# A two-layer encoder trunk on one core, its instruction order planned on another timing simulator

## Chip, cores and metric

The kernel runs on one core of a Trainium2 chip. The metric is the device time of one execution in microseconds (us); the figures below are medians of several runs, and one profiled execution gives the trace. Five engines take instructions, each from a queue of its own and each in the order of that queue: TensorE (PE in the rows; PEld is its weight load), VectorE (DVE), ScalarE (ACT), GpSimd (POOL), and SyncE (SP), which here only issues DMAs. SPq, DVEq and so on in a row are the engine's own instruction queue.

## What is computed

The trunk has two layers over 512 frames of width 1024, in float32. Cut to what matters, for x of shape (512, 1024):

```
for i in (0, 1):
    h = even_mixer(x) if i == 0 else odd_mixer(x, positions)
    x = layer_norm(sqrt(2) * x + h)
    gu = x @ w_gate_up[i];  gate, up = gu[:, :2816], gu[:, 2816:]
    x = layer_norm(sqrt(2) * x + (silu(gate) * up) @ w_down[i])

even_mixer(x):
    p = x @ w_in                             # one projection for both head groups
    a = gated linear attention, 4 heads, chunks of 64 frames, gated state
    b = RWKV-7, 8 heads of 64: S_t = S_{t-1} diag(w_t) + (S_{t-1} a_t) b_t^T + v_t k_t^T, y_t = S_t r_t,
        group norm, bonus term, low-rank output gate
    return concat(a, b) @ w_out

odd_mixer(x, positions):
    q, kv = low-rank projections with rms_norm, rotary key shared by 16 heads
    s = (q k^T) * scale, masked by chunks of 64;  return (softmax(s) v) @ w_out
```

## The kernel before

The program is traced once, in straight line, with no loop on the chip: 21743 instructions in the trace. The tracing library sees tiles (`pool.tile`), works out every semaphore, and at the end orders the instructions itself. Its scheduler walks through a simulated execution: whenever an engine is free there, the engine takes, of the instructions whose inputs and buffers are ready in the simulation, the one that was traced first. So the code's order is a priority, and the simulator's clock decides when a later instruction may pass an earlier one. What comes out is one fixed list for each engine; on the chip nothing passes anything any more within a list. By the library's own description it has two such simulators. The default one leaves out the fixed cost of GpSimd's elementwise instructions; the other, a timeline simulator, is more detailed, and of the activation tables it sees no loads.

All large products are three matmuls each (`gemm3`, lines 185, 186 and 187): each float32 operand is split into a rounded high part (a copy on ScalarE, line 191 or 216) and the rest (VectorE, line 192, or GpSimd), or the rest is built by an accumulating DMA that GpSimd issues (lines 215, 1263 and 1506).

**The first stage** (`even_mixer`) is a set of generators that `weave` interleaves by hand-set costs: the input projections (`gemms`, `proj`: 25 blocks of 128 columns, 24 matmuls each, the matmuls `ps_g<-xh,wh`, `ps_g<-xl,wh`, `ps_g<-xh,wl` of lines 185 to 187), four RWKV streams of two heads each (`rwkv_prep`, `rwkv_chunks`, `rwkv_out`: many 64x64 matmuls, lines 520 to 780), the gated linear attention (`gla_scores` with line 870, `gla_states`, `gla_out`), and the output projection (`w_out`). In `rwkv_prep`, GpSimd multiplies and copies a tile (`e.R`, line 532, and `AR`, line 533). The ScalarE functions of this stage are pinned to table loads by explicit order edges (`behind`).

**The feed-forward stages** (`ffn`, line 1236) multiply by a Strassen-like scheme: for each of six column groups, products P1 to P7, each two token halves wide, whose results VectorE combines (line 1270); `turn` transposes the combined halves (line 1314) before the down projection (`down_ln`, lines 185 to 187 again). **The attention stage** (`mla`) computes scores (line 1617), transposes (line 1633) and value products (line 1646) two units behind one another, with the key and query projections as a background stream. Layer norms end each half layer (`Norm`, lines 1027 to 1036), and the last one writes the output (line 1038).

All pools are opened inside one `ExitStack` in `body`. `body` is called with the tile context open and nothing else is traced in it.

Of the kernel before, what the change touches and what calls it, by code (L numbers as in the profile page):

```python
# [1688 lines left out]
def body(tc, I, O, coff, voff, dbg=False):  # L1689
# [2 lines left out]
    g.table = None  # L1692
    g.nc, g.tc, g.I, g.O, g.dbg = nc, tc, I, O, dbg
    from contextlib import ExitStack
    with ExitStack() as es:
        cp = g.cp = es.enter_context(tc.tile_pool(name="cp", reuse_waits="tile", bufs=1))
        g.dp = es.enter_context(tc.tile_pool(name="dp", bufs=1, space=bass.MemoryType.DRAM))
        cst = cp.tile([P, I["cst"].shape[1]], F32, name="cst")
# [116 lines left out]
```

## Time and profile before

| | |
|---|---|
| median of 3 runs | 1392.69 us (1392.04 to 1393.3) |
| the profiled execution's own time | 1392.04 us |
| its span, first to last instruction | 1390.0 us |
| TensorE busy | 1339.4 us (96%) |
| VectorE busy | 920.7 us (66%) |
| ScalarE busy | 686.5 us (49%) |
| GpSimd busy | 233.4 us (17%) |
| granted TensorE clock, mean | 0.99 |

A matmul's record overlaps the next one's, so that TensorE's busy time says where it waited (busy is missing), and not how fast it ran. Times within the profile count from the first instruction of the span.

### The profile page before, as it was taken

What the parts mean: (1) busy time and instruction counts of PE and PEld (TensorE: products, weight loads), DVE (VectorE), ACT (ScalarE), POOL (GpSimd) and SP (SyncE); (2) the same over time, 40 slices, a digit from 0 to 9 for tenths busy, and PEclk for the clock granted to TensorE, in tenths of its full rate; (3) what the DMA queues carried; (4) which work ended last, traced back from release to release, by engine and by line L of the source; (5) the groups of instructions that cost most, each with busy time, mean ns of one, the idle gap of its engine ahead of it and who ended that gap; (6) DMA issues with size and microseconds to landing.
All of it is one profiled execution on the core that took longest, in us unless ns stands there. A gap on an engine that the chain in (4) does not pass through costs nothing.

```text
span 1390.0 us, 21743 instructions
## 1 busy us (share of the span) xinstructions
PE 1339.4 (96%) x8382; PEld 1060.7 (76%) x8382; DVE 920.7 (66%) x1704; ACT 686.5 (49%) x1212; POOL 233.4 (17%) x278
## 2 busy tenths in 40 slices
PE   8899999999999999999999999999999899999997
PEld 6577777766677788997888877666677788997886
DVE  3687677644496766667556367988785766667456
ACT  6653344455536455555344346555445455555341
POOL 2230021132311111127301220000001111120000
PEclk9999999989999999999999999999999999999999
DMA  7563343531478787763225321111367787773232
GB/s 243 114 125 60 74 100 72 105 65 46 145 221 198 157 189 166 151 125 97 91 93 157 109 94 47 53 55 46 117 163 190 155 193 167 145 127 93 91 107 90
DMA packets 74328, 168.15 MB, mean 121 GB/s; under 512 B 21232, under 2 KB 22384, under 8 KB 74096
## 3 DMA queue, kind: packets, MB, share of 16 engines
q0 software_dynamic: 21888, 60.83, 26.2%
q1 hardware_dynamic: 51808, 103.83, 22.6%
q10 hardware_dynamic: 528, 2.10, 0.4%
q8 instruction: 66, 1.08, 0.3%
q14 instruction: 38, 0.31, 0.1%
HBM read 163.77 MB, written 2.95 MB: 120 GB/s over the span
## 4 chain that ended last, share of the span: by engine, by line
PE 55%; DVE 4%; DMA 4%; issue 4%; ACT 2%; POOL 1%; SPq 0%; DVEq 0%; ACTq 0%; POOLq 0%
PE ps_g L1236 23%; PE ps_g L186 8%; PE ps_g L185 8%; PE ps_g L187 8%; PE ps_s L1617 3%; DMA raw<-in_w_gu 2%; PE ps_o L1646 2%; PE ps_t L1633 1%; PE ps_s L1314 1%; DMA wl<-in_w_mi 1%; DVE wl L192 1%; ACT wh L191 1%; DVE w L1270 0%; DMA w<-in_w_mo 0%; DVE x L1008 0%
## 5 line engine op out<-in xcount | busy, mean ns | idle before, releaser
L192 DVE TENSOR_TENSOR wl<-raw,wh 128x1024 fp32r<-128x1024 f32 (+1 forms) x116 | 127.6, 1111 | 87.7 <-ACT wh L191 87.7
L191 ACT CAST wh<-raw 128x1024 fp32r<-128x1024 f32 (+1 forms) x116 | 111.6, 967 | 140.7 <-PE ps_g L1236 94.9
L1263 POOL DMA_DIRECT2D raw<-in_w_gu x96 | 83.3, 869 | 496.9 <-DVE wl L192 274.0
L1236 PE MATMUL ps_g<-wh,xh 128*128 128x512 f32 (+1 forms) x312 | 115.9, 372 | 2.1 <-ACT wh L191 2.1
L187 PE MATMUL ps_g<-xh,wl 128*128 128x512 f32 (+2 forms) x296 | 113.2, 382 | 3.3 <-DMA wl<-in_w_even 2.2
L1236 PE MATMUL ps_g<-wh,xl 128*128 128x512 f32 (+1 forms) x312 | 114.8, 368 | 0.0
L185 PE MATMUL ps_g<-xh,wh 128*128 128x512 f32 (+2 forms) x296 | 114.6, 387 | 0.0
L186 PE MATMUL ps_g<-xl,wh 128*128 128x512 f32 (+2 forms) x296 | 113.3, 383 | 0.0
L186 PE MATMUL ps_g<-wl,ah 128*128 128x512 f32 x288 | 112.0, 390 | 0.6 <-DVE wl L192 0.6
L185 PE MATMUL ps_g<-wh,ah 128*128 128x512 f32 x288 | 111.7, 392 | 0.5 <-ACT ah L191 0.4
L187 PE MATMUL ps_g<-wh,al 128*128 128x512 f32 x288 | 110.8, 389 | 0.0
L192 DVE TENSOR_TENSOR wl<-w,wh 128x1024 fp32r<-128x1024 f32 (+2 forms) x79 | 89.4, 1132 | 31.9 <-ACT wh L191 31.4
L191 ACT CAST wh<-w 128x1024 fp32r<-128x1024 f32 (+2 forms) x79 | 76.3, 966 | 61.4 <-PE ps_g L186 36.5
L191 ACT CAST ah<-hid 128x512 fp32r<-128x512 f32 x72 | 43.7, 621 | 98.8 <-PE ps_g L186 98.8
L192 DVE TENSOR_TENSOR al<-hid,ah 128x512 fp32r<-128x512 f32 x72 | 49.4, 697 | 60.7 <-ACT ah L191 60.7
L1236 PE MATMUL ps_g<-wh,Sh 128*128 128x512 f32 (+1 forms) x232 | 87.1, 376 | 0.0
L1236 PE MATMUL ps_g<-wh,Sl 128*128 128x512 f32 (+1 forms) x232 | 86.7, 374 | 0.0
L1236 PE MATMUL ps_g<-wl,xh 128*128 128x512 f32 (+1 forms) x312 | 78.2, 372 | 4.1 <-DVE wl L192 4.1
L215 POOL DMA_DIRECT2D wl<-in_w_even x48 | 41.6, 867 | 227.0 <-ACT wl L214 191.9
L216 ACT CAST wh<-w 128x512 fp32r<-128x512 f32 x64 | 39.4, 618 | 81.2 <-PE ps_g L186 49.4
L187 PEld LDWEIGHTS ps_g<-xh,wl 128*128 128x128 f32 (+1 forms) x296 | 55.8, 189 | 14.9 <-DMA wl<-in_w_even 3.4
L1236 PEld LDWEIGHTS ps_g<-wh,xh 128*128 128x128 f32 x312 | 58.6, 188 | 10.6 <-ACT wh L191 3.2
(462 smaller groups left out, 3293.2 us busy)
## 6 DMA issues: line engine op xcount, KB each, us to landing
raw<-in_w_gu POOLq DMA_DIRECT2D x64, 512.0 KB, 5.6
w<-in_w_dn SPq DMA_DIRECT2D x44, 512.0 KB
raw<-in_w_gu SPq DMA_DIRECT2D x32, 512.0 KB
w<-in_w_even SPq DMA_DIRECT2D x48, 256.0 KB
wl<-in_w_even POOLq DMA_DIRECT2D x48, 256.0 KB, 4.7
raw<-in_w_gu POOLq DMA_DIRECT2D x32, 384.0 KB, 4.8
w<-in_w_gu SPq DMA_DIRECT2D x12, 512.0 KB
raw<-in_w_gu SPq DMA_DIRECT2D x16, 384.0 KB
```

Source lines behind the costliest of these rows:

```text
L185: nc.tensor.matmul(out, lhsT=wh, rhs=xh, start=first, stop=False)
L186: nc.tensor.matmul(out, lhsT=wh, rhs=xl, start=False, stop=False)
L187: nc.tensor.matmul(out, lhsT=wl, rhs=xh, start=False, stop=last)
L191: c = nc.scalar.copy(h, src)
L192: (eng or nc.vector).tensor_tensor(l, in0=src, in1=h, op=ALU.subtract)
L215: nc.gpsimd.dma_start(l, src, accum_op=ALU.add)
L216: nc.scalar.copy(h, w)
L1236: nc.tensor.matmul(acc[u][:, :n], lhsT=A_[a][:, k, P * u:P * u + P], rhs=w[:, q], start=first and k + a + b == 0, stop=k + b == 4, skip_gr ...
L1263: nc.gpsimd.dma_start(T[k][k2], w[r, q, k2], accum_op=ALU.add)
L1314: nc.tensor.transpose(out=p[:, m * P:(m + 1) * P], in_=y[:, m * P:(m + 1) * P], identity=g.C("ident"))
L1617: nc.tensor.matmul(p[:, :nk], lhsT=Q[:, h % 4, qb * P:(qb + 1) * P], rhs=K[:, h % 4, :nk], start=True, stop=True)
L1646: nc.tensor.matmul(o[64 * e:64 * e + 64, kb * P:], lhsT=Vv[:, kb, (h - 1 + e) * 64:(h + e) * 64], rhs=t[e][kb][:, kb * P:], start=kb == 0, ...
```

## The change

The whole body of the kernel is traced inside one block, and that block is scheduled on the timeline simulator in place of the default one. By the library's description a block is a basic block of its own, entered unconditionally and scheduled as a unit: nothing traced outside is scheduled in among its instructions. No operation, tile, buffer count or traced order is changed.

```diff
@@ -1692,7 +1692,7 @@
     g.table = None
     g.nc, g.tc, g.I, g.O, g.dbg = nc, tc, I, O, dbg
     from contextlib import ExitStack
-    with ExitStack() as es:
+    with tc.block(schedule_with_timeline_sim=True), ExitStack() as es:
         cp = g.cp = es.enter_context(tc.tile_pool(name="cp", reuse_waits="tile", bufs=1))
         g.dp = es.enter_context(tc.tile_pool(name="dp", bufs=1, space=bass.MemoryType.DRAM))
         cst = cp.tile([P, I["cst"].shape[1]], F32, name="cst")
```

## Rows read from the trace of the kernel before

**Rows 1.** The page's head: span, then busy us, share, instructions of each engine

```profile
span 1390.0 us, 21743 instructions
PE 1339.4 (96%) x8382; PEld 1060.7 (76%) x8382; DVE 920.7 (66%) x1704; ACT 686.5 (49%) x1212; POOL 233.4 (17%) x278
```

**Rows 2.** Busy time by stretches: us, each engine (instructions), TensorE clock, DMA share, GB/s

```profile
34.75:104.25 69.50, 62.11 (x379) 43.95 (x379) 49.32 (x98) 44.02 (x79) 20.36 (x26) 0.98 0.59 120
104.25:278.00 173.75, 168.96 (x2314) 128.61 (x2313) 120.59 (x297) 71.50 (x130) 25.91 (x33) 1.00 0.40 82
278.00:382.25 104.25, 102.49 (x903) 70.01 (x901) 47.76 (x99) 55.33 (x125) 32.09 (x31) 0.94 0.31 86
...
486.50:625.50 139.00, 139.00 (x714) 124.36 (x713) 92.04 (x116) 75.74 (x109) 25.47 (x30) 1.00 0.77 158
...
1112.00:1251.00 139.00, 139.00 (x716) 124.54 (x715) 91.79 (x115) 75.74 (x109) 25.13 (x29) 1.00 0.78 158
```

**Rows 3.** TensorE's waits, 0 to 420 us: who for whom, total us, times, longest

```profile
PE ps_c L520 <- ACT sq L518: 2.7, 1, 2.7
PE ps_l L870 <- DVE lvd L864: 2.2, 4, 1.4
...
PE ps_c L562 <- DVE sq L530: 2.1, 2, 1.8
PE ps_c L562 <- DVE Mrb L554: 1.5, 2, 1.1
PE ps_l L870 <- DVE big L873: 1.0, 1, 1.0
```

**Rows 4.** TensorE's waits, 420 to 1390 us

```profile
PE ps_s L1314 <- DVE w L1270: 7.1, 6, 1.3
```

**Rows 5.** TensorE in order of time, 208.8 to 213 us: start, us, what

```profile
209.35 0.39 PE L185 MATMUL ps_g<-xh,wh 128*128 128x512 f32 x1
211.12 1.15 PE L870 MATMUL ps_l<-lvd 64*64 64x64 f32 x32 [1.39 <-DVE lvd L864]
212.20 0.49 PE L186 MATMUL ps_g<-xl,wh 128*128 128x512 f32 x1
```

**Rows 6.** VectorE in order of time, 206 to 212 us

```profile
205.89 0.42 DVE L863 TENSOR_TENSOR lvd<-gq,lvd 128x256 f32<-128x256 f32 x1
...
208.76 1.46 DVE L863 TENSOR_TENSOR lvd<-gq,lvd 128x256 f32<-128x256 f32 x1
210.15 0.82 DVE L864 TENSOR_TENSOR lvd<-gk,lvd 128x256 f32<-128x256 f32 x1
```

**Rows 7.** GpSimd in order of time, 204 to 214 us

```profile
208.66 1.29 POOL L532 TENSOR_TENSOR W<-rT,W 128x512 f32<-128x512 f32 x1
210.01 0.69 POOL L533 COPY AR<-W 128x512 f32<-128x512 f32 x1
```

**Rows 8.** TensorE in order of time, 456.5 to 461 us

```profile
458.83 0.63 PE L1314 MATMUL ps_s<-cst,w 128*128 128x128 f32 x4 [1.33 <-DVE w L1270]
460.64 0.63 PE L1314 MATMUL ps_s<-cst,w 128*128 128x128 f32 x4 [1.18 <-DVE w L1270]
```

**Rows 9.** Busy time in the stretches where the granted clock was 0.50

```profile
55.14:58.56 3.42, 3.31 (x6) 1.99 (x7) 2.91 (x6) 2.80 (x7) 1.73 (x2) 0.50 0.34 78
277.01:287.25 10.24, 10.24 (x56) 5.53 (x52) 1.16 (x3) 3.83 (x7) 4.76 (x6) 0.50 0.42 66
307.73:311.14 3.41, 3.41 (x32) 2.05 (x26) 1.69 (x2) 0.30 (x1) 2.98 (x3) 0.50 0.41 114
461.33:464.74 3.41, 3.41 (x10) 2.63 (x8) 3.41 (x6) 1.79 (x3) 1.35 (x2) 0.50 0.44 44
1085.97:1089.38 3.41, 3.41 (x10) 2.64 (x8) 3.41 (x6) 1.55 (x3) 1.59 (x2) 0.50 0.46 54
```

**Rows 10.** The projections' matmuls in the first 400 us: duration min/median/max, first and last start

```profile
L187 PE MATMUL ps_g<-xh,wl x192: 387/393/796, 25.0 to 336.1; 128*128 128x512 f32 x192
```

**Rows 11.** The last RWKV stream's gate product, line 780, by the same columns

```profile
L780 PE MATMUL ps_c<-big,big x8: 587/640/692, 140.3 to 356.8; 32*128 32x512 f32 x8
```

**Rows 12.** All engines in order of time: the first load, and the last stores

```profile
0.73 0.40 SPq L282 DMA_DIRECT2D fw<-in_w_even  x1
...
1386.26 0.99 SPq L1038 DMA_DIRECT2D out_x<-x  x2
```

## The prediction, made before the changed kernel was run

> **What bounds the kernel now.** I read the page's head first. TensorE is busy for 1339.4 of 1390.0 us [rows 1], so at most 50.6 us of the span is time in which it did nothing, and no other engine comes near it (VectorE 66%). Then the table of stretches, to see where those 50.6 us lie [rows 2]. The two long feed-forward stretches have none: 139.00 busy of 139.00. The woven first stage has some everywhere: 7.39 us in 34.75 to 104.25, 4.79 in 104.25 to 278, 1.76 in 278 to 382.25. Third, TensorE's waits, to see for whom it stood still: in the first stage for one step of a recurrent stream at a time, a ScalarE square (line 518) or a VectorE product (lines 530, 554, 864, 873), each a few times and none over 2.7 us [rows 3]; later above all the transposes of `turn`, six times for VectorE, 7.1 us [rows 4]. Last the order of time around one of these waits, to see what stood behind it. At 209.35 a projection matmul of line 185 starts, reading `wh`; then the 32 score matmuls of line 870 wait 1.39 us; only behind them comes line 186, which reads the same `wh` and an `xl` that had been there since the first stage began [rows 5]. So TensorE idled with a ready matmul in its queue. That is the only kind of loss which a new order can take away, and the whole argument is how many such losses there are and how many new ones come in.
>
> **The change, part by part.**
>
> *The instructions.* None is added, removed or resized. TensorE's own 1339.4 us stay, but for the clock (below). Nothing that is missing in the 139.00 us stretches can be gained.
>
> *The block itself.* Each engine gets one more jump at the start, and a join at the end. The trace has no such block. At the start everything hangs on the first load, which SP issues at 0.73 us [rows 12]; all that comes before it, the program's own jump included, takes those 0.73 us, so another jump costs between 0 and 0.7. At the end the last two stores take 0.99 us from 1386.26, and 2.8 us are left to 1390.0 for landing, waits and joins; another join is between 0 and 0.7 by the same row. It can't gain. I take 0.5 for both together, nearest to the low end, since 0.73 holds all of the program's own start.
>
> *The order in the first stage.* The priority is the code's in both kernels; what differs is when the simulation calls an instruction ready. The waits that I count as order losses are 2.7 + 2.2 + 2.1 + 1.5 + 1.0 = 9.5 us [rows 3]: a matmul that was let to the front too early, before a step on ScalarE or VectorE that took longer on the chip than in the plan. The clearest has GpSimd in it. The VectorE product of line 863 takes 0.42 us alone and 1.46 us at 208.76, and line 864 0.82 us behind it [rows 6], while GpSimd runs lines 532 and 533 from 208.66 to 210.70 [rows 7]. GpSimd's elementwise cost is what the default simulator leaves out in part. A planner that knows these durations puts the consumers later and lets line 186 pass. The bounds are 0 and 9.5 us of gain. I take half, -4.8: the five rows are of the kind that longer durations mend, but a plan can't know a duration that only a collision makes.
>
> [...]
>
> *The order in the feed-forward stages.* The transposes of line 1314 wait 1.33 and 1.18 us at 457 to 460.6 [rows 8], and the row of waits has six such, 7.1 us in all [rows 4]. Two feed-forward stages of one code make three each; two of the three stand as in rows 8 and stand in front of products of the next column group, so about 2 x (1.33 + 1.18) = 5.0 us could be passed over; the rest, at the last group, has nothing behind it. Bounds 0 and 5.0; half is -2.5.
>
> *The clock.* [...] If half of the waits go, half of 5.1 goes: -2.6; bounds 0 and 5.1.
>
> *New waits.* The plan is still a plan, and the code's costs in `weave` were set by hand around the old one. New waits like those of rows 3 are to be expected: between 0 and as many again, 9.5 us. I take a quarter, +2.4, since TensorE nearly always has some projection matmul ready until 336 us [rows 10].
>
> *ScalarE, SP and GpSimd's DMA issues.* Their order moves too. ScalarE is busy for half of the span and GpSimd for a sixth [rows 1], and TensorE's work covers them; a table load more or less hides there unless a matmul waits for it, and then it counts among the new waits.
>
> **Sum:** 0.5 - 4.8 - 2.5 - 2.6 + 2.4 = -7.0 us. Span 1390.0 - 7.0 = 1383.0; the profiled execution took 2.0 us more than its span (1392.04 against 1390.0), so 1385.0; the median of the runs is 0.65 above that execution, so 1385.7. I say 1386.
>
> **The rivals.**
>
> *Waits swapped for waits.* The feed-forward and attention stages keep their order, since there nearly every instruction is ready in the code's order, and in the first stage as many waits come in as go out. For it: 278 of 1390 us are without a wait [rows 2], and the waits that can go at all are only 9.5 + 5.0 us. Against it: an exact balance is chance. Time 1392 to 1394.
>
> *The cover runs out (slower).* The projections last until 336.1 us and the last RWKV stream until 356.8 [rows 10, 11]: the wide matmuls cover the recurrent chains almost to their end. A plan with longer steps in those chains finds them not ready more often, and fills in projections, which are always ready. Then the projections end earlier, and the last chains run alone. For it: 34.75 to 104.25, where few streams run, idles 7.39 of 69.5 us, 10.6% [rows 2]. At that share the stretch of 278 to 382.25 would idle 11.1 in place of 1.8 us, +9.3; and if the clock fell there for as long again as the 13.65 us of rows 9, +6.8. Time 1392.7 + 16.1 = 1408.8. It decides from the point where the projections end some 40 us early, so that two of the four streams have no cover. Against it: `weave` still sets the priorities.
>
> [...]
>
> *The dense stretches take waits (slower).* In 486.5 to 625.5 and 1112 to 1251 the old order has no wait. If the new one puts VectorE's splits of the next weights ahead of the combinations, `turn` waits as in rows 8. There are four inner column groups with two halves in each of the two stages: 16 places at 1.2 us; half of them give 9.5 us, 1402. It outweighs the gain from the sixth such wait. Against it: the code's order works there as it stands, and is still the priority.
>
> **How the numbers follow.** Chances: the forecast 0.47 (1386, its own range 1378 to 1389), waits swapped 0.19, cover runs out 0.22, dense stretches 0.12. A measurement of this kernel can tell about 0.2%, 2.8 us, from no change. So faster 0.47, same 0.19, slower 0.34. Low end: all 9.5 + 5.0 + 5.1 = 19.6 us gained and nothing lost gives 1373. High end: the dearer slow rival, 1409, and the block's 0.7 twice with it: 1411. That leaves out about one case in six.
>
> **What the profile after would show.** Right: the waits of lines 520, 562 and 870 shorter or gone, line 186 ahead of line 870 where rows 5 have it behind; `turn`'s six waits fewer; the clock at 0.50 in at most two stretches; 139.00 of 139.00 still in the dense stretches; the projections still ending within 10 us of 336. Wrong: projections that end before 300 us and idle time behind them; L1314 waits in the dense stretches; a longer start than 0.73 us to the first load; or GpSimd and VectorE colliding in new places, with VectorE's 256-column products at twice 0.42 us more often than now.

## The result and the profile after

The changed kernel took 1506.18 us (median of four runs, 1502.94 to 1510.0) against 1392.68 us of the kernel before (1392.04 to 1393.3) on the same chip: a ratio of 1.082, 95% interval 1.079 to 1.086. It is slower by 113.5 us, outside the predicted range.

The page's head of the changed kernel (profiled execution 1510.0 us), which answers to [rows 1]:

```profile
span 1508.1 us, 21745 instructions
PE 1379.3 (91%) x8382; PEld 1099.2 (73%) x8382; DVE 919.6 (61%) x1704; ACT 679.6 (45%) x1209; POOL 236.0 (16%) x278
```

The span grew by 118.1 us. TensorE's idle time went from 50.6 to 128.8 us, +78.2; its busy time rose by 39.9 us although it has the same 8382 matmuls. That fits the clock: 138.9 us of busy time lie in stretches at 0.50, against 23.8 before, and at full clock the median records are the same in both kernels (389 ns for a 128x512 matmul, 218 ns for a 64x64 one). The other engines' busy times moved by about 1% or less. The table of stretches, the first three those of [rows 2], the others the first and second feed-forward column loops at their new places:

```profile
34.75:104.25 69.50, 64.45 (x394) 46.10 (x391) 50.05 (x100) 46.35 (x84) 21.48 (x25) 0.98 0.65 133
104.25:278.00 173.75, 161.18 (x2142) 128.65 (x2140) 100.75 (x249) 67.90 (x123) 26.06 (x36) 0.93 0.41 81
278.00:382.25 104.25, 82.09 (x691) 57.54 (x690) 50.49 (x105) 31.88 (x79) 22.98 (x21) 0.69 0.17 39
...
562.50:701.50 139.00, 139.00 (x714) 124.23 (x713) 89.28 (x113) 74.70 (x109) 25.05 (x29) 1.00 0.77 157
1232.00:1371.00 139.00, 137.84 (x708) 122.99 (x706) 88.58 (x112) 74.36 (x109) 25.16 (x30) 1.00 0.76 155
```

The dense loops are all but untouched (139.00 and 137.84 us busy of 139.00). In 34.75 to 104.25 TensorE is even busier than before; the loss opens behind that, and in 278 to 382.25 a fifth of the time is idle, the clock is 0.69 on average and the DMA share has fallen from 0.31 to 0.17. The clock's records show 0.50 for 186.0 us of the span in 19 stretches (before: 27.6 us in six, five of them [rows 9], the sixth at the end); the longest is this one:

```profile
308.30:373.20 64.90, 45.83 (x394) 30.95 (x396) 27.73 (x56) 11.55 (x30) 10.74 (x12) 0.50 0.09 21
```

The projections' matmuls and the last stream's gate product, against [rows 10] and [rows 11]:

```profile
L187 PE MATMUL ps_g<-xh,wl x192: 387/389/794, 25.7 to 296.4; 128*128 128x512 f32 x192
...
L780 PE MATMUL ps_c<-big,big x8: 587/692/1217, 190.0 to 428.9; 32*128 32x512 f32 x8
```

The wide matmuls end 40 us earlier, the recurrent chain 72 us later. TensorE's waits, 0 to 420 us, against [rows 3]:

```profile
PE ps_c L715 <- ACT Mab L739: 9.6, 1, 9.6
PE ps_c L752 <- DVE rT L753: 6.0, 10, 2.3
...
PE ps_l L919 <- DVE SV L913: 5.6, 2, 4.3
PE ps_c L674 <- DVE kT L663: 5.4, 1, 5.4
...
PE ps_c L562 <- DVE Mrb L554: 1.0, 1, 1.0
```

and from 420 us on, against [rows 4]:

```profile
PE ps_g L1236 <- ACT wh L191: 10.0, 7, 2.2
PE ps_g L1236 <- ACT third L191: 9.1, 4, 4.6
...
PE ps_s L1617 <- ACT pr L1623: 4.8, 8, 1.0
PE ps_t L1633 <- ACT PT L1635: 4.5, 7, 2.5
```

Of the waits that the prediction wanted to mend, lines 520 and 870 are gone, line 562 is down to 1.0 us, and line 1314 has no row at all. New ones stand in their place, longer, in the recurrent chains (lines 674 to 752, 919), in the feed-forward stages (line 1236 for ScalarE's weight splits of line 191, 19.1 us in the two rows against 3.8 before) and in the attention (1617, 1633).

Where the 118.1 us lie, by marks that every run below has (first start of VectorE's line 1270, the first feed-forward combination: 447.7 us before, 523.6 after; last start of line 1635, the attention's last copies: 993.4 and 1101.7; end): **A**, first stage up to line 1270, +75.9; **B**, first feed-forward stage and attention, +32.4; **C**, the rest, +9.8. Within B the attention carries it: from the first start of line 1617 to the last of line 1635 it takes 195.6 us against 164.1, with TensorE idle for 17.2 us against 0.2. These marks scatter by a few us: in two runs below that are as fast as the kernel before (the block alone, all five lists as before) A is -3.7 and +2.3.

Attention stretches of equal length, before and then after:

```profile
888.00:963.40 75.40, 75.39 (x345) 49.05 (x346) 64.40 (x208) 41.71 (x116) 1.89 (x1) 1.00 0.18 56
```

```profile
980.20:1055.60 75.40, 65.61 (x255) 38.63 (x255) 54.65 (x173) 32.28 (x91) 1.89 (x1) 0.89 0.11 36
```

**One dependent step, seen closely.** Line 674 multiplies, ScalarE copies the product (line 684), and the next matmul of line 674 reads the copy. In the kernel before, TensorE in order of time, and ScalarE's copy:

```profile
112.31 1.15 PE L674 MATMUL ps_c<-kT,sw 64*64 64x64 f32 x32
113.38 1.12 PE L593 MATMUL ps_c<-y,cst 128*128 128x512 f32 x2
...
113.56 0.59 ACT L684 COPY av<-ps_c 128x512 f32<-128x512 f32 x1 [0.56 <-PE ps_c L674]
...
114.44 0.74 PE L674 MATMUL ps_c<-rT,av 64*64 64x64 f32 x18
```

The same step in the changed kernel:

```profile
126.30 1.15 PE L674 MATMUL ps_c<-kT,sw 64*64 64x64 f32 x32 [1.04 <-DVE kT L681]
127.55 0.58 ACT L684 COPY av<-ps_c 128x512 f32<-128x512 f32 x1 [5.91 <-PE ps_c L674]
...
128.44 1.09 PE L562 MATMUL ps_c<-AR,sq 64*64 64x128 f32 x16 [0.99 <-DVE Mrb L554]
129.46 0.50 PE L187 MATMUL ps_g<-xh,wl 128*128 128x512 f32 x1
...
132.76 0.39 PE L186 MATMUL ps_g<-xl,wh 128*128 128x512 f32 x1
...
133.08 0.62 PE L674 MATMUL ps_c<-rT,av 64*64 64x64 f32 x14
```

The copy took as long (0.58 against 0.59 us). But its reader, which in the old order started 0.3 us after the copy's end, now had its inputs from 128.13 on and started at 133.08, 4.95 us later, behind 16 matmuls of line 562 (which had themselves waited until 128.44) and 15 projection matmuls (129.46 to 132.76). TensorE is busy for all but 0.3 us of that time, so that the view of waits shows next to nothing of the loss. By the reading that the experiments test, it is paid later, when the projections are used up and the chain, late by many such steps, runs alone.

One step is one example. The same delay can be summed over the traces: for each first-stage matmul that waits on a semaphore and does not write the projections' accumulators (`ps_g`), the time from the last event it waits for to its start. Before, it is 184 us over 211 matmuls; in the changed kernel 330 us over 201, of which two matmuls alone have 98. The four streams run side by side, so the sum is a measure of the order and not time lost.

### The profile page after: what moved, and what is told of

Same layout as the page of the kernel before. It is cut to its first block, busy times and chain, and to the rows that moved or that the text cites. A ratio compares the mean times of both kernels' runs of the same rounds, so it can differ in the third digit from the quotient of the medians.

```text
span 1508.1 us, 21745 instructions
## 1 busy us (share of the span) xinstructions
PE 1379.3 (91%) x8382; PEld 1099.2 (73%) x8382; DVE 919.6 (61%) x1704; ACT 679.6 (45%) x1209; POOL 236.0 (16%) x278
## 5 line engine op out<-in xcount | busy, mean ns | idle before, releaser
L1236 PE MATMUL ps_g<-wh,xh 128*128 128x512 f32 (+1 forms) x312 | 119.5, 383 | 14.2 <-ACT wh L191 10.0
L185 PE MATMUL ps_g<-wh,ah 128*128 128x512 f32 x288 | 96.4, 390 | 0.0
L191 ACT CAST ah<-hid 128x512 fp32r<-128x512 f32 x72 | 41.1, 619 | 97.3 <-PE ps_g L186 95.0
L187 PEld LDWEIGHTS ps_g<-xh,wl 128*128 128x128 f32 (+1 forms) x296 | 56.9, 192 | 17.2 <-DMA wl<-in_w_even 6.1
```

What stands on the lines that cost most here:

```text
L185: nc.tensor.matmul(out, lhsT=wh, rhs=xh, start=first, stop=False)
L187: nc.tensor.matmul(out, lhsT=wl, rhs=xh, start=False, stop=last)
L191: c = nc.scalar.copy(h, src)
L1236: nc.tensor.matmul(acc[u][:, :n], lhsT=A_[a][:, k, P * u:P * u + P], rhs=w[:, q], start=first and k + a + b == 0, stop=k + b == 4, skip_gr ...
```

## The experiments

The theory after the result: TensorE's list puts wide matmuls ahead of dependent steps, so that the cover is spent and the chains are late. Rivals: the block itself; the lists of the other engines; the durations that the new simulator assumes. Each run stands beside runs of the kernel before on its own chip (medians 1385.4 to 1388.3 us there, 1392.7 us on the chip of the result), so ratios are compared; a difference in us between runs on two chips carries a few us of that spread.

**The block without the simulator.**

```diff
-    with tc.block(schedule_with_timeline_sim=True), ExitStack() as es:
+    with tc.block(), ExitStack() as es:
```

> The whole body in one block, ordered by the default simulator as before. Theory (TensorE's new order spends its cover, the projections, too early, and the recurrent chains then run alone): the block is no part of it, so the time stays at 1392.7 us, with at most 1 us more for a jump and a join. Rival (the block itself costs, by its start, its join or what it forbids): some tens of us of the 113 appear here, 1410 us or more.

Measured: 1384.03 us, ratio 0.998 (0.996 to 1.000). The block costs nothing that can be told.

**A ladder of lists.** The changed kernel with order edges that pin an engine's list to a recorded one; `pe` holds the matmuls as traced, the table the recorded order as pairs of start and length. The other engines' lists are pinned in the same way, and the first-stage run takes only the matmuls traced in `even_mixer`.

```diff
+    order = [pe[a + i] for a, n in zip(PE_ORDER[::2], PE_ORDER[1::2]) for i in range(n)]
+    for a, b in zip(order, order[1:]):
+        behind(g, b, a)
```

> The block on the timeline simulator as in the change, but TensorE's 6835 matmuls are pinned by order edges (no waits) to the very order of the kernel before; VectorE, ScalarE, GpSimd and SP are ordered by the timeline simulator around that. Theory (the loss lies in TensorE's order): nearly all of the 113.5 us comes back, 1392 to 1405 us, projections ending at about 336 us, half-clock time back to about 30 us. Rival (the loss lies in the order of the other engines, such as weight splits put ahead of chain steps, or GpSimd put where it collides with VectorE): most of the loss stays, 1470 us or more.

Measured: 1459.61 us, ratio 1.051 (1.049 to 1.054). Neither: 46.6 us come back (43 by the ratios), 71 stay. The projections end at 375.3 us, not at 336, and the clock is at 0.50 for 87.1 us, not 30. In VectorE's list a second kind of loss shows. VectorE in order of time in this run:

```profile
97.35 0.69 DVE L496 TENSOR_TENSOR y<-y,sq 128x512 f32<-128x512 f32 x1
103.90 0.69 DVE L663 TENSOR_TENSOR kT<-Dc,cst 128x512 f32<-128x512 f32 x1 [5.86 <-DMA Dct<-do]
104.51 0.74 DVE L525 SCALAR_TENSOR_TENSOR y<-kT,vec,y 128x512 f32<-128x512 f32 x1
...
109.81 1.09 DVE L530 TENSOR_TENSOR sq<-sq,cs 128x512 f32<-128x512 f32 x1
```

and in the kernel before:

```profile
93.81 0.67 DVE L496 TENSOR_TENSOR y<-y,sq 128x512 f32<-128x512 f32 x1
...
94.71 0.73 DVE L525 SCALAR_TENSOR_TENSOR y<-kT,vec,y 128x512 f32<-128x512 f32 x1
...
104.64 0.69 DVE L663 TENSOR_TENSOR kT<-Dc,cst 128x512 f32<-128x512 f32 x1 [1.17 <-DMA Dc<-do]
```

Line 663 reads a round trip through DRAM. Before, VectorE ran line 525 and fifteen others first; here it stands at line 663 for 5.86 us with line 525 behind it, and line 530's consumer on TensorE waits 6.43 us (TensorE's records carry the line of the helper that records the matmuls, 1743):

```profile
111.05 1.34 PE L1743 MATMUL ps_c<-AR,sq 64*64 64x128 f32 x20 [6.43 <-DVE sq L530]
```

Nothing starts on VectorE in those 5.86 us, and line 525 starts at 104.51, 0.61 us behind line 663.

> The mirror of the run above: the default simulator, in a block, with TensorE's matmuls pinned to the order that the changed kernel had; the other engines are ordered by the default simulator around that. Theory (TensorE's order): 1490 to 1515 us, projections ending at about 296 us and about 190 us at the half clock. Rival (the other engines' order): 1395 to 1430 us.

Measured: 1505.3 us, ratio 1.085 (1.082 to 1.088), the time that the theory said. But it is lost in other places: A is +49.6, B +40.9 and C +20.8, the projections end at 278.1 us, not at 296, and the clock is at 0.50 for 146.9 us, not 190. So TensorE's new list, with the default planner's lists fitted around it, is enough for a loss of this size; that it is the same loss is not shown.

> The changed kernel with only the first stage's matmuls pinned to TensorE's order of before; from the first feed-forward stage on TensorE keeps the timeline simulator's order. Theory: the first stage's +68.7 us go and the later +49.4 us of span stay, so 1506.2 - 68.7 = 1437 us, with the attention still 33 us longer than before. If the later stages' loss was only an echo of the late first stage (other buffers free, other loads in flight), it goes too: about 1395 us. Rival (other engines' order): 1490 us or more.

Measured: 1470.4 us, ratio 1.059 (1.054 to 1.063), between the 1437 us of the theory and the 1490 of its rival. Part A is +36.6 in place of +75.9 (the other lists keep the rest), B is +28.1 against 32.4: most of the attention's loss is its own, not an echo of the first stage.

> The block on the timeline simulator, TensorE's and VectorE's lists both pinned to those of the kernel before; ScalarE, GpSimd and SP stay with the timeline simulator. With TensorE alone pinned it was 1459.6 us, 71 us above before. Theory (the other half of the loss is VectorE's list: instructions that read a round trip through DRAM, lines 649 and 663, stand at its head too early, VectorE waits, and what is behind them on VectorE is what TensorE needs): most of the 71 us goes, 1395 to 1415 us. Rival (ScalarE's weight splits, or SP's order of loads): 1440 us or more stays.

Measured: 1425.01 us, ratio 1.028 (1.025 to 1.030), between the two marks: 34.6 of the 71 us are VectorE's list.

> The mirror: only VectorE's list pinned to that of before, TensorE and the rest with the timeline simulator. If the two lists lose the same time twice over (the chains are late in both), one alone mends little: 1470 to 1506 us. If VectorE's list is where the loss begins, and TensorE's order only follows from the plan's late VectorE steps, TensorE's list comes out near that of before and the time falls to 1400 to 1430 us.

Measured: 1559.43 us, ratio 1.124 (1.121 to 1.127): slower than the change, which neither side expected. VectorE's list of before, made for the old TensorE list, under the new TensorE list: A is +97.3. A list is good only together with the others.

> The block on the timeline simulator with TensorE's, VectorE's and ScalarE's lists pinned to those of before; only GpSimd's and SP's are the timeline simulator's. The ladder so far: TensorE alone 1459.6, with VectorE 1425.0. If ScalarE's weight splits hold the rest: 1390 to 1400 us. If SP's and GpSimd's order of loads does: 1410 to 1425 us.

Measured: 1400.13 us, ratio 1.010 (1.007 to 1.013). ScalarE's list is worth 24.9 us, SP's and GpSimd's the rest.

> The block on the timeline simulator with all five lists pinned to those of before. If the change is nothing but the order of five lists: 1385 to 1394 us, no difference that can be told from before. If the block, its barriers or the semaphores that it works out cost something of their own: more than 1395 us.

Measured: 1388.89 us, ratio 1.001 (0.999 to 1.004). The change is the order of five lists and nothing else that can be told. The ladder in one line: 1506.2, TensorE pinned 1459.6, VectorE too 1425.0, ScalarE too 1400.1, all five 1388.9. The share of each list holds for this order of pinning only: VectorE's alone made the time worse.

**The readers of the DRAM round trips.** The 22 edges hold line 663, and line 649 at some of its steps, behind the VectorE instruction that stood ahead of each before (`HOLD` has 22 pairs).

```diff
+    for a, b in zip(HOLD[::2], HOLD[1::2]):
+        g.tc.add_manual_dep(dve[a], dve[b].name, mybir.DependencyInfo(mybir.DependencyClass.NoSync, mybir.DependencyReason.DATA), reason="order")
```

> TensorE's list pinned to that of before, and of VectorE's 1699 instructions only 22 held back: the readers of the round trips through DRAM (line 663, and line 649 where it starts), each behind the VectorE instruction that stood ahead of it in the kernel before. If those early readers are what VectorE's list costs: from 1459.6 down to 1415 us or less. If the loss is spread over the list: above 1440 us.

Measured: 1438.31 us, ratio 1.037 (1.034 to 1.040), between the two marks: 21.3 of the 34.6 us of VectorE's list hang on 22 of its 1699 instructions.

**The cover, held.** The same kind of edge on TensorE, for every eighth projection matmul (66 pairs: projection matmul, chain matmul):

```diff
+    for a, b in zip(HOLD[::2], HOLD[1::2]):
+        g.tc.add_manual_dep(pe[a], pe[b].name, mybir.DependencyInfo(mybir.DependencyClass.NoSync, mybir.DependencyReason.DATA), reason="order")
```

> The changed kernel with 66 order edges: in the first stage every eighth matmul of the projections may not stand ahead of the recurrent-chain matmul behind which it stood in the kernel before. All else is as the timeline simulator orders it. Theory of the spent cover in its plain form (projections that end 40 us early are the loss): projections end at about 335 us again, and most of the first stage's 68.7 us returns, 1440 to 1460 us in all. Rival (the loss is made step by step: dependent matmuls of one chain stand too far apart, whatever fills the place between them): the chains are as late as they were, and 1485 us or more stays.

Measured: 1488.75 us, ratio 1.075 (1.071 to 1.079). The row of the projections in this run:

```profile
L187 PE MATMUL ps_g<-xh,wl x192: 387/393/1415, 24.4 to 378.0; 128*128 128x512 f32 x192
```

They last to 378.0 us, past the old 336.1, and still A is +58.1 of +75.9. So most of the loss does not need the early end of the projections. The plain theory of the spent cover fell here; what remained is the step by step delay.

**Later priority for the projections.**

```diff
-    g.slow = 2.5
+    g.slow = 5.0
```

> The changed kernel with the hand-set cost of a projection block doubled (g.slow 5.0 in place of 2.5), so that the projections are traced later and every chain step that is ready goes ahead of them; window as in the change. If the loss is that the code's priorities fit the other planner only: it falls by tens of us, 1470 us or less. If places are given away before the chain step is ready, a priority can't help, since it counts only among the ready: within 10 us of the change, 1496 to 1516 us.

Measured: 1493.12 us, ratio 1.078 (1.072 to 1.083): 13 us less than the change (6 by the ratios, whose intervals overlap), 3 below the range for "a priority can't help", and far from the 1470 us of its rival. The projections, though traced later, end at 290.1 us, sooner than the 296.4 of the change. By the theory, a priority counts only among instructions that are ready, and the step at 128.13 us was not ready in the plan when its place was given away; no run recorded the plan's own times, so this is argued.

**How early a place is given away.** The timeline simulator has a setting for each engine, by the author's reading the number of instructions that the engine's sequencer may take ahead of the engine in the plan (the expectations call this the window). By the theory of these runs the list is written in the order in which the sequencer takes them, so that what is ready now goes ahead of a dependent step that becomes ready a moment later. The runs change that setting before the trace, and nothing in the program (here to 3; the other runs differ in the number and the engines):

```diff
+    from concourse.hw_specs import TRN2Spec
+    TRN2Spec.ENG_ISSUE_QUEUE_DEPTH = {e: 3 for e in TRN2Spec.ENG_ISSUE_QUEUE_DEPTH}
```

The five, in the order of their expectations: 1 for every engine (by the theory 1388 to 1410 us), 1 for TensorE alone, 1 for all but TensorE, 8 for TensorE alone, 3 for every engine. Where a run names no number the setting is left as the simulator has it, "unset" in the table.

> [...] Nothing of the program is changed, only the order in which it is written down. [...] Rival (the detailed simulator's durations are what misplaces instructions, a transfer through DRAM priced too short above all): the window changes little, 1470 us or more.

> [...] If TensorE's run-ahead is the loss: within 15 us of the run with all at 1. If VectorE's and ScalarE's windows lose on their own what their lists lost under a pinned TensorE (71 us, 35 of it VectorE's): 1430 to 1465 us.

> [...] If TensorE's run-ahead is the loss: it stays, 1480 to 1510 us. If the other engines' windows are: 1400 to 1430 us.

> [...] By the theory the loss grows with the window: between the run with TensorE at 1 and the change, about a quarter of the way up, 1415 to 1445 us. If it is one step (any run-ahead at all loses everything), 1480 us or more.

> [...] At 3 a load may still be handed over beside a running matmul in the plan, which at 1 it could not. Theory (run-ahead spreads the dependent steps; the run with 1 failed because its plan took TensorE for far slower than it is): the time goes on falling from the 1475.0 us of TensorE's window 8, to 1415 to 1450 us. Rival (any change of the window only distorts, and 8 was luck): above 1475 us.

| TensorE / others | us | ratio (95%) | A | B | C | from line 684's copy to its reader, first three streams |
|---|---|---|---|---|---|---|
| default simulator, before | 1392.68 | 1 | 0 | 0 | 0 | 0.30, 0.05, 1.41 us |
| unset / unset, the change | 1506.18 | 1.082 (1.079 to 1.086) | +75.9 | +32.4 | +9.8 | 4.95, 4.84, 0.93 us |
| unset / 1 | 1488.08 | 1.072 (1.066 to 1.077) | +56.3 | +31.4 | +5.5 | |
| 8 / unset | 1475.03 | 1.062 (1.056 to 1.067) | +57.5 | +20.4 | +4.2 | 0.61, 0.05, 1.43 us |
| 3 / 3 | 1441.89 | 1.041 (1.039 to 1.044) | +40.0 | +12.1 | +2.5 | 0.05, 0.05, 0.88 us |
| 1 / 1 | 1650.3 | 1.188 (1.182 to 1.195) | +180.8 | +71.0 | +9.8 | 4.45, 0.30, 0.05 us |
| 1 / unset | 1673.1 | 1.205 (1.199 to 1.211) | +179.8 | +69.7 | +33.6 | |

Of the five expectations two came out, those of unset / 1 and of 3 / 3; 8 / unset stayed 30 us above its range, and with TensorE at 1 the time rose. From the change to 8 / unset and 3 / 3 it falls, by 64 of 113 us in all (half of the loss by the ratios), and the dependent step closes up. No run has 3 for TensorE alone, so what TensorE's setting gives between 8 and 3 is not separated from the other engines'. The step of line 684 with 3, from the views of TensorE and ScalarE in order of time:

```profile
126.62 1.15 PE L674 MATMUL ps_c<-kT,sw 64*64 64x64 f32 x32 [0.56 <-DVE T L651]
127.70 0.50 PE L187 MATMUL ps_g<-xh,wl 128*128 128x512 f32 x1
...
127.88 0.59 ACT L684 COPY av<-ps_c 128x512 f32<-128x512 f32 x1 [2.84 <-PE ps_c L674]
...
128.51 0.27 PE L674 MATMUL ps_c<-rT,av 64*64 64x64 f32 x2
```

At 3 the projections end at 344.3 us and at 8 at 334.7, as late as before, with A at +40.0 and +57.5: once more the end of the cover does not tell the loss. Nor does the one step of line 684: at 8 / unset it is as close as before, with A at +57.5. The sum over the first stage's dependent matmuls, 184 us before and 330 with the change, is 252 at 8 / unset and 158 at 3 / 3: there it is less than before, and A is still +40.0, so what is left at 3 / 3 is no such delay on TensorE. My expectation for 1 was wrong by 240 us. There the projections last to 497.9 us, and the page's row of engines shows TensorE idle for 225.7 of 1651.6 us:

```profile
PE 1425.9 (86%) x8382; PEld 1108.9 (67%) x8382; DVE 937.6 (57%) x1704; ACT 689.2 (42%) x1213; POOL 222.2 (13%) x278
```

On the chip loads stand beside matmuls (PE and PEld add up to 2534.8 us in that row, in a span of 1651.6). A plan in which they may not would have TensorE far slower than the chip's, and would put steps in front that come too early; this was argued, not shown.

> The planner's window at 3 for every engine, as in window_all_3 (1441.9 us), and with it the 22 order edges that keep the readers of the DRAM round trips (line 663, and line 649 where it starts) behind the VectorE instructions that stood ahead of them in the kernel before. VectorE's waits for these transfers were 17 us at line 663 there. If they are the remainder: 1415 to 1427 us. If they are a symptom (VectorE would have nothing else to do at those moments): within 8 us of 1441.9.

Measured: 1445.04 us, ratio 1.041 (1.036 to 1.045): no gain over 1441.89. VectorE's waits at lines 649 and 663 for these transfers fell only from 22.1 to 13.7 us, and the total did not fall. Under this order they are a symptom, though under TensorE's order of before they were worth 21 us.

**What stays open.** The last 54 us with a setting of 3: 40.0 in the first stage, 12.1 in the feed-forward and attention part. Whether they come from durations that the plan assumes or from a list built greedily around another timing was not separated. Nor is the run-ahead isolated as the cause of the half that came back: the setting may move more of the plan than that, for at 1 the time rose to 1650.3 us. In the attention no experiment of its own was made; that it answers to the same setting (B +32.4, +20.4, +12.1 unset, at 8 and at 3) is all that is shown.

## Why the prediction was wrong, point by point

- **What bounds the kernel.** Right that only idle time and the clock can move: +78.2 and +39.9 us make up the 118.1. But I read "TensorE idled with a ready matmul in its queue" [rows 5] as the only kind of loss that an order makes. The larger kind leaves no idle time where it arises: a ready dependent step behind work that could have come later.
- **The premise of the sum** was that "the priority is the code's in both kernels; what differs is when the simulation calls an instruction ready". It failed. The runs point to a third thing: how long before its start an instruction's place is fixed. Doubling the projections' cost gave 13 us at most, cutting the run-ahead to 3 gave 64.
- **The block, +0.5.** Right: no cost that can be told, first load at 0.73 us as before.
- **Order in the first stage, -4.8, and in the feed-forward stages, -2.5.** The waits went as forecast, and more: of 9.5 us [rows 3] 1.0 is left, and line 1314's 7.1 us [rows 4] are gone. At the place of rows 5 projection matmuls now fill the time until line 870 starts at 210.00, and line 863's 1.46 us are gone: its longest is 455 ns (line 864 still takes 0.83 us once). That gain of up to 15.6 us is buried by the rest; how much of it the longer durations gave, and how much the other order as such, was not separated. The list of waits had left out the largest of that window, line 185 for ScalarE's `xh` (5.4 us before, 5.6 after); it did not move.
- **New waits, +2.4: the step that failed.** Its reason, that "TensorE nearly always has some projection matmul ready", was true, and by the runs on the run-ahead it was much of the harm: whatever is ready is put ahead of what is about to be. TensorE idled 73.0 us in the first stage (472.2 less 399.24 busy) against 21.2 before (403.5 less 382.31), so waits gone and waits come make +51.8 us there, and +17.0 in the attention, where the sum had +2.4 for all new ones. The bound of 9.5 us "as many again" counted waits of an order whose dependent steps stood close; it says nothing of an order in which they don't.
- **The clock, -2.6.** Wrong in sign: 186.0 in place of 27.6 us at 0.50, and 39.9 us more busy time in place of 2.6 less. No run shows the 5.1 us of which the -2.6 is half: the waits of lines 520 and 1314 went, and the time at 0.50 grew. The rival's +6.8 us takes half of 13.65 us, which was the author's estimate; what the traces show of work at 0.50 stands in the last section. The two longest stretches, 64.9 us from 308.3 and 34.1 us from 403.9, lie behind the last projection matmul (296.4), where the chains run alone.
- **The cover runs out.** The right side, the right sign on the profile (projections ending 40 us early, exactly the point from which it was to decide) and the wrong price: 16.1 us against 68.7 up to the first matmul of line 1236 (403.5 before, 472.2 after). I priced the last two streams without cover. In fact the first stream was already 49.7 us late at its gate product (190.0 against 140.3 [rows 11]), with the projections still running. Its cause was wrong as well: with the projections lasting past 336 us A was still +58.1. So its sign came out largely by another cause, which is luck.
- **Dense stretches take waits.** Wrong: 139.00 and 137.84 busy of 139.00, and no wait of line 1314.
- **ScalarE, SP, GpSimd covered at 0.** Wrong: with TensorE's and VectorE's lists as before, the other three lists still cost 36.1 us (1425.0 less 1388.9).
- **Two sums** are off by less than 1 us: half of 16 places at 1.2 us is 9.6, and 1408.8 with twice 0.7 is 1410. Nothing hangs on them.

## What to carry to other kernels

A scheduler that fixes an instruction's place well before it runs can fill the gaps of dependent chains with whatever is ready, and here a more detailed simulator did not mend that. Such a loss need show in no wait where it arises, so measure how long the inputs of a chain's steps have been ready when they start; and where that is as short as before, as at 3 / 3 here, look elsewhere for the rest. Ask of a planner when it decides, not only what it assumes for durations. And a kernel tuned by hand around one planner's lists is tuned for all five lists together: one list put back alone can be worse than none.

## What the runs showed of the hardware that was not expected

- The granted clock stayed at 0.50 for 64.9 us on end (308.3 to 373.2), with TensorE busy for 45.83 of them, 390 of 394 matmuls there being smaller than 128x512; it fell at the end of a wait of TensorE's, 2.13 us for VectorE. In 34.75 to 104.25, where wide projection matmuls run among the small ones, it was 0.98. Records at 0.50 are longer, but not twofold in the median: 311 against 218 ns for a 64x64 matmul of the changed kernel, 628 against 389 ns for a 128x512 one. Records overlap, though: from the start of one to the start of the next of its shape the medians are 427 against 227 ns for 128x512 and 213 against 109 ns for 128x128, nearly twofold. Line 780's longest, 1217 ns, is from another such stretch (427.9 us), 692 ns at full clock.
- VectorE's 1704 instructions took the same busy time under both planners (920.7 and 919.6 us), and of its 92 products of 256 columns with two inputs the longest took 1461 ns before and 826 ns after. Those over 467 ns, two before (1461 and 824) and one after (826), each have a GpSimd record beside them; the median of all that have one is 417 ns before and 418 after, of those that have none 418 and 415. So for these products the collisions on which part of the prediction hung did not get worse. Over all of VectorE's instructions, 10 before and 13 after had a GpSimd record beside them and took over 0.2 us more than the median of their operation, tiles and shape, by 6.5 and 8.6 us in all.
